# Two-layer hybrid decoder trunk on one core: a later start for the first adding transfers, and two more FFN pairs by seven products

## The chip, the core and the metric

The kernel runs on one core of a Trainium2 chip. The time is device time of one execution in microseconds (us), median of three runs. A core has a matrix engine (TensorE, PE in the profile), a vector engine (VectorE, DVE), a scalar engine (ScalarE, ACT), a general engine (GpSimd, POOL) and a queueing engine (SyncE, SP). Each takes its instructions in its own order and waits on semaphores for the others. Sixteen DMA engines move data; transfers are issued from SP, ACT or POOL, and each of these has a queue of its own on the DMA engines: q1 in the profile is SP's, q10 ACT's, q0 POOL's.

## The reference

x is 512 tokens by 1024 columns, float32. Layer 0 runs latent attention (8 heads) and differential attention (4 heads) in parallel, layer 1 dilated and stick-breaking attention. Each layer ends in a gated convolutional FFN with 2816 hidden columns:

```python
def conv_ffn(h, w_up, conv_w, conv_b, w_down):
    u = causal_dwconv(h @ w_up, conv_w, conv_b)
    gate, up = jnp.split(u, 2, axis=-1)
    return (jax.nn.silu(gate) * up) @ w_down

for i in range(DEPTH):                      # DEPTH = 2
    h = rms_norm(x, pre_g)
    h = even_mixer(h, ...) if i % 2 == 0 else odd_mixer(h, ...)
    x = x + rms_norm(h, post_g)
    h = conv_ffn(rms_norm(x, ffn_pre_g[i]), ...)
    x = x + rms_norm(h, ffn_post_g[i])
```

## The kernel before, in words

**Products.** A float32 operand is split into a high part (a cast to the matrix engine's rounded float32, on ACT) and a low part (the difference, on DVE). A product is three matmuls: high by high, high by low, low by high (`mm3`, lines 315 to 317). For weights these are `wh` and `wl` (lines 81 and 82), made from a raw tile `wraw`. SP loads the raw tiles (lines 57 and 59) in the order of one long list of units, into three buffers; a load waits until the low part of the unit three places earlier is made, for that frees its buffer.

**The stages in order.** `even()`: the combined projections; the latent attention (scores at line 1111, masked by adding `mmask` in the same DVE instruction that finds the maximum, line 895; exponentials on ACT, line 899), with the value products `av` of the differential attention put between its steps; then the differential attention (scores 1227, `alibi` added at 1231, exponentials 1238, combination 1243 to 1245, transposes 906, output 1256, and a normalisation on POOL, 1262 and 1263), with projections for its later heads (`aqk`) as fillers between its steps; then the output projection. `ffn(0)`, `odd()` and `ffn(1)` follow.

**What the differential attention needs first.** When the latent attention's last output is split, ACT issues three loads: `subg` (line 1182), `lamb` (1184) and `alibi` (1188). DVE scales `subg` (1199), forms the lambda sums from `lamb` (1192), then makes the low parts of three weight tiles (82), and then takes the first scores with `alibi` (1231). In ACT's order the first exponentials (1238) stand behind a cast of one more weight tile. The order of these engines in this stage is written out by hand, step by step: score, at most one weight unit, exponentials, fillers, transposes of the step before, output of the step before that.

**The FFN's up product.** The 2816 hidden columns are 22 tiles of gate and up each, worked as 22 pairs. A pair is done directly (two units of weights, 48 matmuls of 512 columns) or, for the pairs in `SEVEN`, by a scheme of seven products of half-size blocks in place of eight (`seven`, 84 matmuls of 256 columns). The scheme needs sums of weight blocks. These sums are not made by the engines but by **adding transfers**: DMAs from DRAM to DRAM, issued by POOL, that copy a block or add it to what is there. A chunk of three pairs takes eight of them, each waiting for those that it builds on:

```python
steps = [(0, 3, ALU.bypass), (2, 2, ALU.bypass), (0, 2, ALU.add), (2, 0, ALU.add), (1, None, ALU.bypass),
         (1, 0, ALU.add), (3, -1, ALU.bypass), (3, 1, ALU.add)]                       # line 161 issues
moves = [lambda c=c, step=step: move(c, *step) for step in steps for c in chunks]
if mark is not None:
    moves.insert(0, lambda: nc.gpsimd.dma_start(tiles[0][chunks[0]][0:1, 0:1], mark)) # line 168
```

A group of moves has no engine that it would naturally wait for. To hold it back until a given moment, `make_sums` puts a **mark** ahead of it: a transfer of one element from a tile that is made at that moment, into the place that the first move overwrites. POOL then waits for the mark's source, and the first move for the mark's landing.

**Where the groups stand.** Chunks 0 to 2 of the first FFN: one group of 24 moves of 768 KB, marked by a normalisation factor of the combined projections (`rk`, line 1074). Chunks 3 and 4: one move after each step of the differential attention. Chunks of the second FFN: one group in `odd()` (line 1494), marked by `lead`. The first FFN has 14 pairs by seven (4 to 17), the second 12 (4 to 15, four chunks). In the stretch by seven the orders of PE, DVE and ACT are written out by hand (line 633 on); a weight unit is made some two to three units ahead of its use.

The tile framework chooses the order of the instructions where no hand-written order is given, from its own estimates, before the kernel runs.

Of the kernel before, what the change touches and what calls it, by code (L numbers as in the profile page):

```python
# [33 lines left out]
PAIRED = [f for k in range(HF) for f in (k, HF + k)]  # L34
TAIL = 4

SEVEN = range(4, 18), range(4, 16)
CHUNK = 3
PAIRS = [len(n) for n in SEVEN]
CHUNKS = [-(-n // CHUNK) for n in PAIRS]  # L40
# [55 lines left out]
def trunk(tc, A, out):  # L96
    nc = tc.nc
    PE, ACT, DVE, POOL = nc.tensor, nc.scalar, nc.vector, nc.gpsimd

    with ExitStack() as top:  # L100
# [28 lines left out]
        lead = cst.tile([P, 80], F32, tag="lead", name="lead")  # L129
# [15 lines left out]
        def sum_steps(layer, chunks, mark=None):  # L145

            wide = "(a q) c -> a (q c)"
            if layer not in sums_of:
                sums_of[layer] = [[dpool.tile([CHUNK * P, S], F32, tag=f"ws{layer}{j}{c}", name="ws")
                                   for c in range(CHUNKS[layer])] for j in range(4)]  # L150
            tiles = sums_of[layer]

            def move(c, j, src, op):
                n = min(CHUNK, PAIRS[layer] - c * CHUNK) * P
                if src is None:
                    src = tiles[0][c][:n]
                elif src < 0:
                    src = tiles[1][c][:n]
                else:
                    src = A[f"ffn_up_q{layer}"][src, c * CHUNK * P:c * CHUNK * P + n]  # L160
                nc.gpsimd.dma_start(tiles[j][c][:n].rearrange(wide, q=4), src.rearrange(wide, q=4), accum_op=op,
                                    max_dma_last_dim=8192)

            steps = [(0, 3, ALU.bypass), (2, 2, ALU.bypass), (0, 2, ALU.add), (2, 0, ALU.add), (1, None, ALU.bypass),
                     (1, 0, ALU.add), (3, -1, ALU.bypass), (3, 1, ALU.add)]
            moves = [lambda c=c, step=step: move(c, *step) for step in steps for c in chunks]
            if mark is not None:
                moves.insert(0, lambda: nc.gpsimd.dma_start(tiles[0][chunks[0]][0:1, 0:1], mark))
            return moves

        def make_sums(layer, chunks, mark):
            with tc.manual_schedule(engines={POOL.engine}):
                for move in sum_steps(layer, chunks, mark):
                    move()
# [13 lines left out]
        def ffn_units(layer):  # L188
            up = []
            for f in range(NF):  # L190
                if f == SEVEN[layer][0]:
                    up += up_blocks(layer)
                elif f not in SEVEN[layer]:
                    up += [(A["ffn_w_up"][layer, f, z], 1024) for z in range(2)]
# [203 lines left out]
        def ffn(layer, xnT, pending, final):  # L398
            with ExitStack() as es:
# [3 lines left out]
                nc.sync.dma_start(cw[:], A["ffn_conv"][layer])  # L403
                pairs = SEVEN[layer]
                minus = cw[:, pairs[0]:pairs[-1] + 1:pairs.step, 1, 0:3]
# [22 lines left out]
                early, hold, homes = [], {}, {}  # L428
# [26 lines left out]
                def x_block(k0, t0):  # L455
                    return [x[:, k0:k0 + 4, t0:t0 + 256] for x in (xh, xl)]
# [91 lines left out]
                def more():  # L548
                    nonlocal ready
                    ready += 1  # L550
                    W.ahead(min(ready, stop))
# [9 lines left out]
                def seven(n, last):  # L561


                    u = begun
                    y = sp.tile([P, 2, S], F32, tag="y", name="y")
                    z1, z2 = u[0][:, :256], u[0][:, 256:]
                    c21, c22 = u[1][:, :256], u[1][:, 256:]
                    p5 = y[:, 1, :256]
                    scale, conv, silu, rest = last
                    heavy = len(rest) > 1  # L570

                    conv(0)
                    more()
                    scale(1)
                    p = bank("t", "p5")[:, :256]
                    product(p, sums[0], True)
                    ACT.copy(p5, p)
                    silu()
                    if heavy:
                        conv(1)  # L580
                    else:
                        more()
                    product(z1, x_block(4, 0), False)
                    product(c21, sums[1], False)
                    DVE.tensor_tensor(z2, c21, p5, ALU.add)
                    if heavy:
                        rest[0]()
                    else:
                        conv(1)
                    more()  # L590
                    if n != pairs[-1]:
                        begin_seven()
                    if heavy:
                        rest[1]()
                    product(c21, sums[2], False)
                    DVE.tensor_tensor(c22, c21, p5, ALU.add)
                    rest[2 if heavy else 0]()
                    product(z2, x_block(4, 256), False)
                    more()
                    product(c21, sums[3], False)  # L600
                    if heavy and n < 2 * (HF - 4) + 2:
                        rest[3]()
                    elif heavy:
                        late.append(rest[3])
                    left = evict(n, y, u)
                    left[0](0)
                    return left
# [14 lines left out]
                for n, f in enumerate(PAIRED):  # L622
                    if n == 2:
                        for i in ORDER:
                            nc.sync.dma_start(spill[i * P:(i + 1) * P, :], X[i][:])
                    if n == (2 if final else 3):
                        for step in x_sums():
                            step()
                    if n == pairs[0]:
                        depth, W.depth = W.depth, 0  # L630
                        ready, stop = W.pos + 3, W.pos + (7 * PAIRS[layer] + 1) // 2 + 2
                        W.ahead(ready)
                        written = tc.manual_schedule(engines={PE.engine, DVE.engine, ACT.engine})
                        written.__enter__()
                        begin_seven()
                    if n in pairs:
                        left = seven(n, left)
                        if n == pairs[-1]:
                            for step in late:
                                step()  # L640
                            finish(left)
                            written.__exit__(None, None, None)
                            W.depth = depth
                        continue
                    u = u4[2 * n:2 * n + 2] if n < 2 else [None] * 2
                    y = sp.tile([P, 2, S], F32, tag="y", name="y")
                    scale, conv, silu, rest = left = evict(n, y, u)
                    for z in range(2):
                        if u[z] is None:
                            u[z] = bank("as"[z], "u")  # L650
                            wh, wl = W.next()
                            for k in range(KD):
                                b = slice(k * P, (k + 1) * P)
                                mm3(u[z], wh[:, b], wl[:, b], xh[:, k], xl[:, k], k == 0, k == KD - 1)
                        if z == 0 or n != pairs[0] - 1:
                            scale(z)
                        if n != pairs[0] - 1:
                            conv(z)
                    if n != pairs[0] - 1:
                        silu()  # L660
                        for step in rest:
                            step()
# [199 lines left out]
        def even():  # L862
            with ExitStack() as es:
# [51 lines left out]
                with ExitStack() as e1:  # L915
# [116 lines left out]
                    with ExitStack() as e2:  # L1032
# [11 lines left out]
                        for i in ORDER:  # L1044
# [9 lines left out]
                            rk = mean_square(a[:, 256:384])  # L1054
# [16 lines left out]
                            split(cT[0][:, :, t], cT[1][:, :, t], tp[:, 0:3])  # L1071
                            ACT.copy(mk[0][64:128, t], tp[64:128, 3])
                            ACT.copy(mk[1][0:64, t], tp[0:64, 3])
                        make_sums(0, range(3), rk[0:1, 0:1])
                        for z in range(2):
                            diff_qk(0, z)
                        ch, cl = cT
# [25 lines left out]
                    sc = e1.enter_context(tc.tile_pool(name="esc", bufs=1, reuse_waits="tile"))  # L1103
                    mmask = sc.tile([P, S], F32, tag="mmask", name="mmask")
                    nc.scalar.dma_start(mmask[:], A["mla_mask"])

                    def score(p2, i, z):
                        def f(_):
# [299 lines left out]
        def odd(xnT, pending, order):  # L1408
            xh, xl = xnT
            with ExitStack() as es:  # L1410
# [80 lines left out]
                DVE.tensor_copy(tri[:], trif[:])  # L1491

                ACT.copy(lead[0:1, 1:2], st[0:1, 0:1])
                make_sums(1, range(CHUNKS[1]), lead[0:1, 1:2])


                for u in range(2):
# [327 lines left out]
def layout(inputs):  # L1825
# [50 lines left out]

    for n, pairs in enumerate(SEVEN):
        q = r["ffn_w_up"][n, pairs[0]:pairs[-1] + 1].reshape(len(pairs), 2, P, 2, S)
# [48 lines left out]
```

## Time and profile before

| | us |
|---|---|
| median of 3 runs | 1135.01 (1134.89 to 1135.72) |
| the profiled execution, its own time | 1134.86 |
| its span, first to last instruction | 1133.1 |
| PE busy | 1115.9 |
| DVE busy | 889.1 |
| ACT busy | 631.5 |
| POOL busy | 108.1 |
| mean granted clock of PE | 0.995 |

In the profile, a row of a timeline reads: start in us from the span's first instruction, duration in us, engine, line, operation, tile written <- tiles read, shapes, count, and in brackets the idle time of the engine before it with what ended it. SPq, ACTq and POOL rows with DMA_DIRECT2D are the issuing of transfers. A row of DMA issues gives the tiles, the queue, the count, the size of one and the median time from issue to landing. A row that begins with a stretch A:B gives its length and the busy time of each engine in it.

### The profile page before, as it was taken

What the parts mean: (1) busy time and instruction counts of PE and PEld (TensorE: products, weight loads), DVE (VectorE), ACT (ScalarE), POOL (GpSimd) and SP (SyncE); (2) the same over time, 40 slices, a digit from 0 to 9 for tenths busy, and PEclk for the clock granted to TensorE, in tenths of its full rate; (3) what the DMA queues carried; (4) which work ended last, traced back from release to release, by engine and by line L of the source; (5) the groups of instructions that cost most, each with busy time, mean ns of one, the idle gap of its engine ahead of it and who ended that gap; (6) DMA issues with size and microseconds to landing.
All of it is one profiled execution on the core that took longest, in us unless ns stands there. A gap on an engine that the chain in (4) does not pass through costs nothing.

```text
span 1133.1 us, 17611 instructions
## 1 busy us (share of the span) xinstructions
PE 1115.9 (98%) x6576; PEld 957.3 (84%) x6576; DVE 889.1 (78%) x1504; ACT 631.5 (56%) x1070; POOL 108.1 (10%) x213
## 2 busy tenths in 40 slices
PE   9979999999999999999999999999999999999997
PEld 8856677789999998888888877888999999888886
DVE  6657566489899999898974476677889999779896
ACT  5445466455566665456653455565466666435662
POOL 2312023320000000000031111102000000000002
PEclk9989999999999999999999999999999999999999
DMA  8799658743355655354637999922236565334461
GB/s 297 268 242 269 183 173 211 176 145 97 118 185 177 195 175 166 98 157 158 227 118 241 313 279 282 281 67 87 98 110 189 184 183 188 113 89 145 147 204 75
DMA packets 66229, 201.48 MB, mean 178 GB/s; under 512 B 9056, under 2 KB 10208, under 8 KB 59360
## 3 DMA queue, kind: packets, MB, share of 16 engines
q1 hardware_dynamic: 56352, 142.09, 38.6%
q0 software_dynamic: 7872, 54.53, 18.7%
q10 hardware_dynamic: 1920, 3.74, 1.1%
q8 instruction: 52, 0.85, 0.3%
q14 instruction: 33, 0.27, 0.1%
HBM read 192.95 MB, written 60.85 MB: 224 GB/s over the span
## 4 chain that ended last, share of the span: by engine, by line
PE 90%; issue 3%; DMA 3%; POOL 1%; DVE 1%; ACT 1%; SPq 0%; POOLq 0%; DVEq 0%; ACTq 0%
PE u L317 12%; PE u L315 12%; PE u L316 12%; PE acc L315 6%; PE acc L317 6%; PE acc L316 6%; PE apt L315 3%; PE apt L316 3%; PE apt L317 2%; PE sps L1111 2%; PE ao L317 1%; PE ao L315 1%; PE ao L316 1%; PE av L317 1%; PE av L316 1%
## 5 line engine op out<-in xcount | busy, mean ns | idle before, releaser
L81 ACT CAST wh<-wraw 128x1024 fp32r<-128x1024 f32 x237 | 245.4, 1048 | 149.0 <-PE u L316 51.3
L82 DVE TENSOR_TENSOR wl<-wraw,wh 128x1024 fp32r<-128x1024 f32 x237 | 287.2, 1219 | 50.7 <-ACT wh L81 50.0
L315 PE MATMUL u<-xh,wh 128*128 128x256 f32 (+1 forms) x664 | 212.0, 319 | 0.0
L316 PE MATMUL u<-xl,wh 128*128 128x256 f32 (+1 forms) x664 | 211.8, 319 | 0.0
L317 PE MATMUL u<-xh,wl 128*128 128x256 f32 (+1 forms) x664 | 211.7, 319 | 0.0
L315 PEld LDWEIGHTS u<-xh,wh 128*128 128x128 f32 x664 | 126.5, 191 | 9.0 <-ACT wh L81 0.3
L317 PEld LDWEIGHTS u<-xh,wl 128*128 128x128 f32 x664 | 126.5, 190 | 8.9 <-DVE wl L82 0.3
L316 PEld LDWEIGHTS u<-xl,wh 128*128 128x128 f32 x664 | 126.5, 190 | 8.7
L317 PE MATMUL acc<-wh,gl 128*128 128x512 f32 (+1 forms) x250 | 96.9, 388 | 0.0
L316 PE MATMUL acc<-wl,gh 128*128 128x512 f32 (+1 forms) x250 | 96.8, 387 | 0.0
L315 PE MATMUL acc<-wh,gh 128*128 128x512 f32 (+1 forms) x250 | 96.8, 388 | 0.0
L317 PE MATMUL u<-gh,wl 128*128 128x256 f32 x312 | 88.3, 283 | 0.0
L315 PE MATMUL u<-gh,wh 128*128 128x256 f32 x312 | 88.3, 283 | 0.0
L316 PE MATMUL u<-gl,wh 128*128 128x256 f32 x312 | 88.3, 283 | 0.0
L230 POOL TENSOR_TENSOR rv<-ms,epst 128x1 f32<-128x1 f32 x39 | 12.1, 309 | 756.0 <-ACT junk L282 369.7
L492 ACT ACTIVATE y<-u,cw 128x512 f32<-128x512 f32 x88 | 67.5, 776 | 14.9 <-PE u L317 14.9
L496 DVE SCALAR_TENSOR_TENSOR y<-u,cw,y 128x511 f32<-128x511 f32 x88 | 65.0, 743 | 5.1 <-ACT y L492 5.1
L498 DVE SCALAR_TENSOR_TENSOR y<-u,cw,y 128x510 f32<-128x510 f32 x88 | 65.5, 746 | 2.3
L315 PEld LDWEIGHTS u<-gh,wh 128*128 128x128 f32 x312 | 59.9, 192 | 0.2
L316 PEld LDWEIGHTS u<-gl,wh 128*128 128x128 f32 x312 | 59.9, 192 | 0.1
L317 PEld LDWEIGHTS u<-gh,wl 128*128 128x128 f32 x312 | 59.9, 192 | 0.0
L315 PEld LDWEIGHTS acc<-wh,gh 128*128 128x128 f32 x250 | 46.9, 188 | 10.1 <-issue 0.5
(363 smaller groups left out, 2437.4 us busy)
## 6 DMA issues: line engine op xcount, KB each, us to landing
ws<-in_ffn_up_q POOLq DMA_DIRECT2D x48, 768.0 KB, 15.3
wraw<-ws SPq DMA_DIRECT2D x104, 256.0 KB, 2.9
wraw<-in_ffn_w_down SPq DMA_DIRECT2D x44, 512.0 KB, 3.5
wraw<-in_ffn_up_q SPq DMA_DIRECT2D x78, 256.0 KB, 2.9
wraw<-in_ffn_w_up SPq DMA_DIRECT2D x36, 512.0 KB, 4.1
ws<-ws POOLq DMA_DIRECT2D x16, 768.0 KB, 16.0
wraw<-in_od_w_dqk SPq DMA_DIRECT2D x12, 512.0 KB, 11.0
wraw<-in_ffn_w_down SPq DMA_DIRECT2D x22, 256.0 KB, 2.9
```

The lines of the kernel that those rows point to most:

```text
L81: self.nc.scalar.copy(h[:, :w], raw[:, :w])
L82: self.nc.vector.tensor_tensor(l[:, :w], raw[:, :w], h[:, :w].bitcast(F32), ALU.subtract)
L230: POOL.tensor_tensor(v[:, :n], ms, epst[:, :n], ALU.add)
L315: PE.matmul(o, lh, rh, start=first, stop=False, skip_group_check=more)
L316: PE.matmul(o, lh, rl, start=False, stop=False, skip_group_check=more)
L317: PE.matmul(o, ll, rh, start=False, stop=last, skip_group_check=more)
L492: ACT.activation(y[:, z], u[z], AF.Identity, bias=c[:, 3:4], scale=c[:, 2:3])
L496: DVE.scalar_tensor_tensor(y[:, z, 1:], u[z][:, :S - 1], c[:, 1:2], y[:, z, 1:], ALU.mult, ALU.add)
L498: DVE.scalar_tensor_tensor(y[:, z, 2:], u[z][:, :S - 2], c[:, 0:1], y[:, z, 2:], ALU.mult, ALU.add)
L1111: PE.matmul(s_ps[:, :w], mq[h][:, i * P:(i + 1) * P], mk[h][:, :w], start=True, stop=True)
```

## The change

Three edits. The first group of adding transfers is marked by the latent mask, when its load has landed, in place of the normalisation factor, and so stands at a later place of the program. The second FFN takes 14 of its pairs by seven products, and so has a fifth chunk (two pairs, moves of 512 KB). The sums of this chunk are made during the first FFN's up product, after its pair 9, marked by an element of a held product that is copied by ACT; the group in `odd()` keeps chunks 0 to 3.

```diff
-SEVEN = range(4, 18), range(4, 16)
+SEVEN = range(4, 18), range(4, 18)
...
                     if n in pairs:
                         left = seven(n, left)
+                        if n == 9 and not final:
+                            ACT.copy(lead[0:1, 2:3], hold[3][0][0:1, 0, 0:1])
+                            make_sums(1, range(4, 5), lead[0:1, 2:3])
                         if n == pairs[-1]:
...
                             ACT.copy(mk[1][0:64, t], tp[0:64, 3])
-                        make_sums(0, range(3), rk[0:1, 0:1])
                         for z in range(2):
                             diff_qk(0, z)
...
                     nc.scalar.dma_start(mmask[:], A["mla_mask"])
+                    make_sums(0, range(3), mmask[0:1, 0:1])
...
                 ACT.copy(lead[0:1, 1:2], st[0:1, 0:1])
-                make_sums(1, range(CHUNKS[1]), lead[0:1, 1:2])
+                make_sums(1, range(4), lead[0:1, 1:2])
```

## The prediction

> **What bounds the kernel now.** I read the page first: TensorE (PE) is busy for 98% of the span and makes up 90% of the chain that ended last.
>
> ```profile
> span 1133.1 us, 17611 instructions
> PE 1115.9 (98%) x6576; PEld 957.3 (84%) x6576; DVE 889.1 (78%) x1504; ACT 631.5 (56%) x1070; POOL 108.1 (10%) x213
> PE 90%; issue 3%; DMA 3%; POOL 1%; DVE 1%; ACT 1%; SPq 0%; POOLq 0%; DVEq 0%; ACTq 0%
> ```
>
> So an edit counts by the PE time that it removes, or by a wait of PE that it ends or makes. Next I read the chain in order of time around the first edit, the timeline of PE there, and a table of stretches (us, PE busy, PEld, DVE, ACT, POOL, granted clock, DMA share, GB/s).
>
> ```profile
> 61.47 11.02 DMA mmask<-in_mla_mask
> ...
> 73.02 2.07 PE L1111 MATMUL sps<-mk,mq 128*128 128x256 f32 x4 [6.83 <-DVE st L895]
> ...
> 66.20:73.00 6.80, 0.00 (x0) 0.00 (x0) 0.34 (x3) 0.00 (x0) 1.33 (x2) 0.87 1.02 261
> 73.00:78.00 5.00, 4.98 (x11) 3.40 (x12) 2.77 (x15) 2.49 (x10) 1.03 (x2) 0.50 1.06 259
> ...
> 75.00:126.00 51.00, 50.91 (x246) 32.45 (x244) 36.51 (x147) 27.61 (x88) 6.51 (x10) 0.97 0.92 237
> 143.00:200.00 57.00, 57.00 (x300) 40.61 (x299) 37.63 (x112) 37.89 (x111) 17.23 (x35) 1.00 0.72 194
> ```
>
> The load of the latent mask takes 11.0 us, PE stands still for 6.8 us behind it, and then works for 5 us at half its clock. The DMA engines are full (1.02) all that time. The rest of the latent attention (75 to 126) and the differential attention (143 to 200) are filled with PE work to the last 0.1 us. The cause is the first group of adding transfers, which POOL issues from 40.05 on:
>
> ```profile
> 36.48 0.75 POOL L168 DMA_DIRECT2D ws<-rr  x1 [0.33 <-POOL rr L233]
> 40.05 3.28 POOL L161 DMA_DIRECT2D ws<-in_ffn_up_q  x6 [2.82 <-DMA ws<-rr]
> 112.61 0.79 POOL L161 DMA_DIRECT2D ws<-in_ffn_up_q  x1 [1.86 <-DMA ws<-ws]
> 149.14 0.19 POOL L1262 TENSOR_TENSOR st<-st,epsp 128x1 f32<-128x1 f32 x1 [35.63 <-ACT jk L1260]
> ```
>
> How the queues share the engines is in the DMA view of short windows (packets, MB, share of the 16 engines' time): first 40 to 125 us (the whole group, on q0), then 65 to 71 (mask on q10, weights on q1), 115.5 to 123 (adds alone), 85.5 to 88 (copies alone).
>
> ```profile
> q0 software_dynamic: 2688, 18.88, 85.3%
> ...
> q0 software_dynamic: 128, 0.89, 71.6%
> q1 hardware_dynamic: 111, 0.45, 20.4%
> q10 hardware_dynamic: 124, 0.25, 10.9%
> ...
> q0 software_dynamic: 205, 1.41, 90.9%
> ...
> q0 software_dynamic: 142, 0.98, 95.8%
> ```
>
> Three things follow. The group needs 0.853 x 85 = 72.5 us of all 16 engines. The three queues got about the same number of packets (128, 111, 124), whatever their size: turn by turn, one packet each. And an adding packet is slow: 7.5 x 16 x 0.909 us over 1.41 MB, that is 172 packets of 8 KB, gives 0.63 us, a copying one 2.5 x 16 x 0.958 over 120 gives 0.32 us. So a small transfer pays one 0.32 to 0.63 us packet of the group for each of its own. The mask (144 packets, 9 on each engine) took nine turns of 0.79 us (0.63 + 0.16), 7.1 us, and 3.9 us of start and landing.
>
> **Edit 1, the group begins at the mask's landing: what it gives.** The same kind of load on the same queue without the group is the smask row; three loads of dqk weights stand beside the mask in either kernel.
>
> ```profile
> smask<-in_sb_mask ACTq DMA_DIRECT2D x1, 256.0 KB, 2.6
> ```
>
> Issued at 61.47, the mask lands at 64.1, or by 65.7 if it takes turns with the weights. PE has value products until 66.2 anyway, so the whole wait of 6.8 us goes, and with it the slow clock: 5.0 us at 0.50 cost at most 2.5, and I take 2.0, since PE had short waits in there. The latent attention then runs **8.8 us earlier**. What is late next in it is PE's own work (the row of 75 to 126).
>
> **What it takes.** POOL's mark now waits for the mask. Behind it in POOL's order stand the 24 moves, a memset and the first normalisation of the differential attention (149.14). By the first two POOL rows, the first move comes 3.6 us after the mark: at 68.0 instead of 40.05. The group then needs its 72.5 us, so it runs until 140.5 at least. In before it was over 1.5 us ahead of the loads of the next stage (last move at 112.61 plus 12.0 to its landing); now these are inside it. This is the transition, first by engine (ACT, DVE, SP, PE), then the landing times of the loads and q10's packets from 126 to 134:
>
> ```profile
> 126.08 0.34 ACTq L1182 DMA_DIRECT2D subg<-in_ev_subln_g  x1
> 136.74 1.05 ACT L81 CAST wh<-wraw 128x1024 fp32r<-128x1024 f32 x1 [2.27 <-DMA wraw<-in_ev_w_dqk]
> 131.60 0.23 DVE L1192 CUSTOM_DVE_ANT_0 lj<-lamb 128x64 f32<-128x64 f32 x1 [2.43 <-DMA lamb<-in_ev_lam]
> 132.02 3.49 DVE L82 TENSOR_TENSOR wl<-wraw,wh 128x1024 fp32r<-128x1024 f32 x3
> 135.50 0.68 DVE L1231 CUSTOM_DVE_ANT_0 s<-sps,alibi 128x512 f32<-128x512 f32 x1
> 139.70 0.75 DVE L1245 SCALAR_TENSOR_TENSOR s<-s,st 128x512 f32<-128x512 f32 x1
> 133.26 0.33 SPq L59 DMA_DIRECT2D wraw<-in_ev_w_dqk  x1
> 140.41 0.92 PE L1227 MATMUL sps<-dqk 64*128 64x384 f32 x4
> 142.75 0.60 PE L906 MATMUL tpp<-ident,s 128*128 128x128 f32 x4
> ...
> alibi<-in_alibi ACTq DMA_DIRECT2D x1, 1024.0 KB, 7.1
> wraw<-in_ev_w_dqk SPq DMA_DIRECT2D x1, 512.0 KB, 3.5
> lamb<-in_ev_lam ACTq DMA_DIRECT2D x1, 128.0 KB, 5.1
> ...
> q10 hardware_dynamic: 432, 1.25, 53.3%
> ```
>
> In before the order is: lamb lands (131.57), DVE goes on to the low parts of the weights (132.02), the first of these frees a raw buffer, SP loads the next weights (133.26 to 136.72), ACT casts them (136.74), and only behind that cast, in ACT's order, come the first exponentials; DVE combines until 140.45, and PE transposes at 142.75, with 2.3 us to spare.
>
> In after the ACT loads are issued at 126.08 - 8.8 = 117.3 and start after about 3.1 us (the mask's 3.9 less its landing), at 120.4. The group has then had 52 us, less some 3 of starts and gaps: 23 us of it are left, which by its order are some ten packets of adds, 18 of copies and 18 of adds on each engine. q10's 432 packets are 27 turns on each engine, with 0.533 x 8 = 4.3 us of its own. lamb is through after 18 turns: 10 x 0.63 + 8 x 0.32 + 1.3 = 10.2 us, with landing at 131; a count with the group 1 us further on gives 129.5. I take 130.5. alibi: nine turns more, 136 to 137. The weights' load is issued 1.7 us after lamb as before, at 132.2, and meets the adds. Loads of that size took 9.8 to 10.9 us beside the group:
>
> ```profile
> wraw<-in_ev_w_dqk SPq DMA_DIRECT2D x1, 512.0 KB, 9.8
> ...
> wraw<-in_ev_w_dqk SPq DMA_DIRECT2D x1, 512.0 KB, 10.9
> ```
>
> With 9.9 it lands at 142.1. Cast to end of combine is 140.45 - 136.74 = 3.7, so PE transposes at 145.8, **3.1 us later** than in before although it came 8.8 earlier. alibi at 136.5 lets DVE's L1231 end at 138, which is ahead of 140.41, so it is not the last gate. PE idles in two pieces, together over 10 us, so the slow clock comes back: +2.0 (0 to 2.5). The row of 143 to 200 has PE full, so nothing is caught up there. Sum of edit 1: **+5.1**, from -8.8 (nothing is held up) to +8 (load 12 us, full dip).
>
> By the Trainium skill ("DMA: Bandwidth & Descriptors", section "Queues, rings and completion order") an engine drains a whole packet of some 9 to 17 descriptors from one ring before it turns to the next. By that rule the small loads would wait for one move's share at a time. The equal counts from 65 to 71 us speak against it; it is the second rival.
>
> **Edit 2, 14 pairs by seven products.** The second FFN's rows (first and last start of the seventh-product matmuls, four to a pair; and of every third matmul of a direct pair):
>
> ```profile
> L315 PE MATMUL p<-gh,wh x48: 283/283/283, 836.0 to 948.0; 128*128 128x256 f32 x48
> L315 PE MATMUL u<-xh,wh x93: 389/389/395, 957.5 to 1020.3; 128*128 128x512 f32 x93
> ```
>
> A pair by seven: (112.0 - 1.1)/11 = 10.08 us. A direct pair is 16 triples of 62.8/92 = 0.683: 10.92. Two pairs: **-1.7 us**. The first FFN does the same 14 pairs now, with PE never idle, so neither weights nor evictions are the limit:
>
> ```profile
> 290.00:433.00 143.00, 143.00 (x1185) 142.41 (x1184) 130.43 (x183) 91.08 (x124) 0.00 (x0) 1.00 0.58 179
> ACT wh L81 <- DMA wraw<-ws: 3.1, 7, 0.7
> ws<-in_ffn_up_q POOLq DMA_DIRECT2D x6, 512.0 KB, 6.8
> ```
>
> **Edit 3, the fifth chunk in the first FFN's up.** One tiny copy on ACT, which is idle for a third of that stretch and whose source was made a pair earlier; one mark and eight moves of 512 KB on POOL, which does nothing there (0.00) until the FFN's tail. At about 6 us each in sequence they run 40 us from about 352. Engine time: four copies of 1.3 and four adds of 2.5. A weight load that meets an add is late by up to 2.5; seven such loads made ACT wait already (at most 0.7) and PE lost nothing. But DVE has only 9% free. I take **+0.5**, from 0 to four adds less DVE's free time, 10 - 3.5, of which I carry +3.
>
> **Sum.** The profiled execution took 1134.86 us, 1.8 more than its span and 0.15 under the median. 1134.9 + 5.1 - 1.7 + 0.5 = **1138.8 us**.
>
> **Rivals.** (a) *Break-even.* The gate at lamb and weights takes up just the 8.8 us: the load lands by 139 (lamb at 129, the load in 8.5 us because the group pauses between its steps), PE transposes at its old time, and only 1.7 less 0.5, plus 0 to 2 of slow clock, remain: 1133.7 to 1135.7. For it: each landing is uncertain by 2 us. Against: the adds fall on the load itself. (b) *Faster.* The loads pass the group: whole moves alternate with whole loads, lamb waits for about 3.8 + 1.9 and the weights for one move; 2 of the 8.8 are lost and no dip comes: 1134.9 - 6.8 - 1.7 + 0.5 = 1127; with nothing held up 1125. It decides if lamb lands before 126. Against: the equal counts and mask's 11.0. (c) *Much slower.* The group stretches so far that POOL's last move, 112.61 + 28 = 140.6, slips past the normalisations (149.14 + 3): every us over 8 is paid by PE; 1143 to 1147. That the mask is still late is unlikely (turns of 0.25 us beside weights alone).
>
> **How the numbers follow.** Forecast 0.50 (own range 1136 to 1142, a fifth of it within 2.3 us of before), (a) 0.22, (b) 0.20, (c) 0.08. A measurement of this kernel can tell about 0.2%, 2.3 us, from no change. Faster: 0.20. Same: (a) and that fifth, 0.32. Slower: 0.48. The range leaves out (c) and most of (b): 1128.0 to 1142.5.
>
> **What would show it.** Edit 1's gain: the mask lands within 4.5 us, PE has no wait of 6.8 us and no half clock near 66. Its price: lamb takes over 10 us from issue, the next weights' load some 10, PE waits for over 8 us before the first transposes of the differential attention, with a half clock behind it. Edit 2: the second FFN's p rows number 56, 10.08 us apart. Edit 3: PE's busy time between 290 and 433 stays whole. The forecast fails if lamb or the weights' load land as fast as alone (5.1 and 3.5), or if DVE takes the weights' low parts ahead of lamb.

## The result

| kernel | time, us (median, range) | ratio to before, 95% interval |
|---|---|---|
| before | 1134.95 (1134.45 to 1135.72, 4 runs) | |
| after | 1143.7 (1142.16 to 1145.82, 4 runs) | 1.0078 [1.0058, 1.0098] |

The change makes the kernel 8.8 us slower. The prediction said slower, 1138.8 us, but its range ended at 1142.5. The profiled execution of after is its fastest run, 1142.16 us, 7.3 more than the profiled one of before. Line numbers of after are up to three higher than those of before.

The page of after, the first two of the three lines that the prediction shows:

```profile
span 1140.3 us, 17809 instructions
PE 1117.0 (98%) x6648; PEld 960.9 (84%) x6648; DVE 893.7 (78%) x1511; ACT 634.8 (56%) x1078; POOL 114.1 (10%) x222
```

PE's busy time is almost the same (1115.9 before), so the 7 us are waits and slower matmuls. The view that names them is the table of waits of PE alone, from 60 to 1100 us (total, times, longest). First before, where the next one is 0.3 us, then after:

```profile
PE sps L1111 <- DVE st L895: 6.8, 1, 6.8
```

```profile
PE sps L1230 <- DVE st L1234: 6.0, 1, 6.0
PE tpp L909 <- DVE s L1248: 4.2, 1, 4.2
PE u L315 <- DVE u L596: 2.2, 1, 2.2
PE u L315 <- DVE u L585: 0.6, 2, 0.4
PE u L315 <- ACT u L559: 0.5, 1, 0.5
```

The wait for the mask is gone. In its place stand two waits at the start of the differential attention (10.2 us together) and four in the first FFN's up (3.3). The first two are edit 1, and this is their timeline in after (POOL, then DVE, SP and ACT, then PE):

```profile
64.79 0.75 POOL L168 DMA_DIRECT2D ws<-mmask  x1 [28.32 <-DMA mmask<-in_mla_mask]
68.38 3.19 POOL L161 DMA_DIRECT2D ws<-in_ffn_up_q  x6 [2.84 <-DMA ws<-mmask]
...
138.84 0.79 POOL L161 DMA_DIRECT2D ws<-in_ffn_up_q  x1 [2.38 <-DMA ws<-ws]
...
130.83 0.23 DVE L1195 CUSTOM_DVE_ANT_0 lj<-lamb 128x64 f32<-128x64 f32 x1 [3.34 <-DMA lamb<-in_ev_lam]
...
131.25 3.49 DVE L82 TENSOR_TENSOR wl<-wraw,wh 128x1024 fp32r<-128x1024 f32 x3
...
132.50 1.47 SPq L59 DMA_DIRECT2D wraw<-in_ev_w_dqk  x2
...
142.83 1.04 ACT L81 CAST wh<-wraw 128x1024 fp32r<-128x1024 f32 x1 [11.26 <-DMA wraw<-in_ev_w_dqk]
...
137.35 2.31 PE L1230 MATMUL sps<-dqk 64*128 64x384 f32 x4 [5.97 <-DVE st L1234]
146.68 1.08 PE L909 MATMUL tpp<-ident,s 128*128 128x128 f32 x4 [4.16 <-DVE s L1248]
```

The chain reads from top to bottom. The mask lands before 64.79, POOL begins the group at 68.38 and issues its last move at 138.84 instead of 112.61. DVE stands for lamb until 130.83, and what it makes next in its order, the low parts of three weight tiles, comes only then (131.25). The first of them frees a raw buffer, so that the next load of weights is issued at 132.50; it lands and is cast at 142.83, and PE transposes at 146.68 instead of 142.75. The stretches of after around this chain (length, PE, PEld, DVE, ACT, POOL, granted clock, DMA share, GB/s) show the clock:

```profile
131.00:137.30 6.30, 0.38 (x2) 0.00 (x0) 4.49 (x12) 0.20 (x1) 1.62 (x2) 0.88 1.02 366
137.30:140.00 2.70, 2.65 (x5) 1.41 (x6) 0.66 (x3) 0.00 (x0) 0.90 (x2) 0.50 1.04 249
...
142.50:146.70 4.20, 0.04 (x2) 0.05 (x1) 2.53 (x5) 2.95 (x6) 0.00 (x0) 0.91 1.01 254
146.70:150.00 3.30, 3.30 (x12) 2.55 (x12) 1.80 (x7) 2.74 (x6) 0.00 (x0) 0.58 1.03 259
```

PE is idle twice, and each time it comes back at about half of its clock, with the DMA engines full (1.01 to 1.04 in these rows) throughout. The loads by their issue rows in after, from 116 to 136 us (count, size, us from issue to landing):

```profile
alibi<-in_alibi ACTq DMA_DIRECT2D x1, 1024.0 KB, 18.4
wraw<-in_ev_w_dqk SPq DMA_DIRECT2D x2, 512.0 KB, 12.8
...
lamb<-in_ev_lam ACTq DMA_DIRECT2D x1, 128.0 KB, 13.5
```

In before these took 7.1, 3.5 and 5.1. (12.8 is the median of two loads; the one of the chain, issued first, was there after 10.3 us.) The third place is the first FFN's up. The same stretch as in the prediction, now in after, and the waits of ACT for weights there (293 to 442 us):

```profile
290.00:433.00 143.00, 139.71 (x1135) 137.94 (x1134) 127.64 (x179) 87.30 (x122) 5.85 (x9) 1.00 0.64 196
```

```profile
ACT wh L81 <- DMA wraw<-ws: 11.7, 6, 4.2
```

PE loses 3.3 us in a stretch that was full, and ACT's longest wait for a weight load has grown from 0.7 to 4.2 us. Edit 2 shows as the prediction had it, 56 rows of seventh products, (132.1 - 1.1)/13 = 10.08 us apart:

```profile
L315 PE MATMUL p<-gh,wh x56: 282/283/284, 845.0 to 977.1; 128*128 128x256 f32 x56
```

By the starts of the first matmuls of each stage, the profiled run of after loses 4.9 us up to the first FFN's up, 4.1 in it, nothing from its down to the second FFN, and wins 1.5 in the second FFN's up.

### The profile page after: what moved, and what is told of

The parts are those of the page before. It is cut to its first block, busy times and chain, and to the rows that moved or that the text cites. A ratio compares the mean times of both kernels' runs of the same rounds, so it can differ in the third digit from the quotient of the medians.

```text
span 1140.3 us, 17809 instructions
## 1 busy us (share of the span) xinstructions
PE 1117.0 (98%) x6648; PEld 960.9 (84%) x6648; DVE 893.7 (78%) x1511; ACT 634.8 (56%) x1078; POOL 114.1 (10%) x222
## 4 chain that ended last, share of the span: by engine, by line
PE 89%; DMA 4%; DVE 3%; issue 1%; ACT 1%; POOL 0%; SPq 0%; POOLq 0%; DVEq 0%; ACTq 0%
PE u L317 11%; PE u L315 11%; PE u L316 11%; PE acc L315 6%; PE acc L316 6%; PE acc L317 6%; PE apt L315 3%; PE apt L316 3%; PE apt L317 2%; PE ao L315 2%; PE ao L317 2%; PE ao L316 2%; PE sps L1114 2%; DMA wraw<-ws 1%; PE aqk L315 1%
## 5 line engine op out<-in xcount | busy, mean ns | idle before, releaser
L315 PE MATMUL u<-xh,wh 128*128 128x256 f32 (+1 forms) x656 | 206.4, 315 | 0.0
L317 PE MATMUL u<-xh,wl 128*128 128x256 f32 (+1 forms) x656 | 206.4, 315 | 0.0
L316 PE MATMUL u<-xl,wh 128*128 128x256 f32 (+1 forms) x656 | 206.3, 314 | 0.0
L315 PE MATMUL u<-gh,wh 128*128 128x256 f32 x336 | 95.6, 284 | 3.3 <-DVE u L596 2.2
L317 PE MATMUL u<-gh,wl 128*128 128x256 f32 x336 | 95.1, 283 | 0.0
L316 PE MATMUL u<-gl,wh 128*128 128x256 f32 x336 | 95.1, 283 | 0.0
L315 PEld LDWEIGHTS u<-gh,wh 128*128 128x128 f32 x336 | 64.4, 192 | 4.2 <-ACT wh L81 2.3
L316 PEld LDWEIGHTS u<-gl,wh 128*128 128x128 f32 x336 | 64.4, 192 | 0.1
L317 PEld LDWEIGHTS u<-gh,wl 128*128 128x128 f32 x336 | 64.4, 192 | 0.0
L161 POOL DMA_DIRECT2D ws<-in_ffn_up_q x60 | 43.1, 721 | 130.2 <-DMA ws<-ws 58.8
```

What stands on the lines that cost most here:

```text
L315: PE.matmul(o, lh, rh, start=first, stop=False, skip_group_check=more)
L316: PE.matmul(o, lh, rl, start=False, stop=False, skip_group_check=more)
L317: PE.matmul(o, ll, rh, start=False, stop=last, skip_group_check=more)
```

## The experiments

My theory after the result: edit 1 costs what the prediction said, edit 2 gives what it said, and the term that was mis-sized is edit 3, because the eight moves delay weight loads in a stretch that has no slack. The rivals: edit 1's late group also spoils the later up; or the moves cost their price in any place; or it is the issuing and the small ACT copy, not the transfers. For all kernels one table, from the starts of the first matmul of each stage in the profiled runs (us): when the first FFN's up begins; how long it takes to the down's first matmul; from there to the second FFN's up; that up to its down.

| kernel | time | up begins | first up | down and odd stage | second up |
|---|---|---|---|---|---|
| before | 1135.0 | 243.5 | 232.2 | 311.8 | 233.5 |
| after | 1143.7 | 248.4 | 236.3 | 311.8 | 232.0 |
| edit 1 alone | 1141.2 | 251.1 | 231.9 | 311.8 | 233.5 |
| edits 2 and 3 alone | 1138.7 | 243.4 | 236.8 | 311.9 | 232.0 |
| fifth chunk in the odd stage | 1144.0 | 243.1 | 232.3 | 322.6 | 232.0 |
| fifth chunk after the seven | 1135.1 | 243.3 | 231.9 | 313.2 | 232.0 |
| fifth chunk in the down | 1139.0 | 244.3 | 231.7 | 318.2 | 232.0 |
| fifth chunk at the start | 1133.4 | 244.3 | 231.9 | 312.1 | 232.1 |
| fifth chunk of copies | 1134.7 | 244.2 | 233.6 | 312.2 | 232.1 |
| lamb early | 1136.7 | 245.1 | 232.4 | 311.7 | 233.6 |
| mask early | 1127.8 | 236.9 | 232.1 | 311.9 | 233.6 |
| mask early, chunk at the start | 1125.7 | 235.8 | 232.3 | 312.4 | 232.0 |

Where nothing ahead of the up was changed, it begins at 243.1 to 244.3; so much a profiled run differs from the next before the places that matter here.

### Edit 1 alone

```diff
-                        make_sums(0, range(3), rk[0:1, 0:1])
...
                     nc.scalar.dma_start(mmask[:], A["mla_mask"])
+                    make_sums(0, range(3), mmask[0:1, 0:1])
```

> Edit 1 alone: the first group of adding moves is marked by the mask's landing; the second FFN keeps 12 pairs by seven and nothing is added in the first FFN's up. Theory: edit 1 and the fifth chunk's sums cost about the same and add up. The first FFN's first direct up matmul comes 4.6 us later than before (273.7 instead of 269.0 in the profiled run), its up takes 206.6 us as before, the second FFN's up 208.2 as before, and the time is 1135.0 + 4.6 = about 1139.6 us. Rival 1, that the first FFN's up is long because of something that edit 1 leaves behind (a later start of the weights, a lower clock): the up takes about 211 us here too, and the time is about 1145. Rival 2, that edit 1 costs nothing by itself: 1135.

Measured: 1141.22 us (1139.70 to 1142.03), ratio 1.0050 [1.0033, 1.0067], that is 3.7 to 7.6 us. The theory's 1139.6 is 1.6 too low. The first FFN's up takes no longer than before, so rival 1 falls; rival 2 falls too. The profiled run has the same chain as after with the lambda load another 2.5 us longer (16.0 us), and its up begins 7.6 us late instead of 4.9. So edit 1 costs 5 to 8 us, and its size differs from run to run with the landing of one small load.

### Edits 2 and 3 alone

```diff
-SEVEN = range(4, 18), range(4, 16)
+SEVEN = range(4, 18), range(4, 18)
...
+                        if n == 9 and not final:
+                            ACT.copy(lead[0:1, 2:3], hold[3][0][0:1, 0, 0:1])
+                            make_sums(1, range(4, 5), lead[0:1, 2:3])
...
-                make_sums(1, range(CHUNKS[1]), lead[0:1, 1:2])
+                make_sums(1, range(4), lead[0:1, 1:2])
```

> Edits 2 and 3 alone: 14 pairs by seven in the second FFN, the fifth chunk's sums inside the first FFN's up, the first group back behind the normalisations where it was before. Theory: the first direct up matmul is at 269 as before, the first FFN's up takes 206.6 + 4.4 = 211 us, the second FFN's up 208.2 - 1.5 = 206.7, and the time is 1135.0 + 4.4 - 1.5 = about 1137.9 us. Rival: the first FFN's up is long because of edit 1; then it takes 206.6 here and the time is about 1133.5.

Measured: 1138.67 us (1137.81 to 1139.98), ratio 1.0034 [1.0021, 1.0047]. The up is 4.6 us longer without edit 1, and the second up 1.5 shorter. The parts add up: 6.1 and 3.6 make 9.7 against 8.8 measured for both, within the intervals.

### Where the eight moves stand: odd stage, end of the seven, down, start

Each of the next four kernels is edits 2 and 3 alone with the fifth chunk's sums at another place. In the odd stage (the group there keeps all five chunks, so the diff is edit 2 only):

```diff
-SEVEN = range(4, 18), range(4, 16)
+SEVEN = range(4, 18), range(4, 18)
```

> Edit 2 alone: 14 pairs by seven in the second FFN, all five chunks of their sums in the odd stage's one group, first group as before. Theory: what edit 3 costs is its place in the first FFN's up. The first FFN's up takes 206.6 us as before, the second FFN's up 206.7, and the time is 1135.0 - 1.5 = about 1133.5 us, if eight more moves in the odd stage's group hold no load up there. Rival: the eight moves cost the same wherever they stand, since they take the queues' time from loads in the odd stage as well: the odd stage becomes 2 to 4 us longer and the time is 1136 to 1138.

Measured: 1144.02 us, ratio 1.0081 [1.0065, 1.0096]. The theory fell here: the moves cost 10.8 us in the odd stage, more than anywhere else. The timeline of PE and SP's rows of that kernel, and SP's rows of before:

```profile
754.89 3.65 PE L1680 MATMUL t<-ident,s 128*128 128x128 f32 x16 [8.21 <-DVE s L1670]
...
733.42 0.33 SPq L1652 DMA_DIRECT2D stat<-st  x1
747.78 0.38 SPq L1653 DMA_DIRECT2D on<-stat  x1
```

```profile
733.79 0.33 SPq L1652 DMA_DIRECT2D stat<-st  x1
738.47 0.38 SPq L1653 DMA_DIRECT2D on<-stat  x1
```

A softmax statistic goes through DRAM there, a store of 16 KB and a load that waits for its landing. In before the group's last move was issued at 718.7, and the store took 4.7 us; in this kernel POOL still issued at 733.8, the store takes 14.3, and PE stands for 8.2 us.

After the last of the fourteen pairs by seven:

```diff
                             finish(left)
+                            if not final:
+                                ACT.copy(lead[0:1, 2:3], hold[3][0][0:1, 0, 0:1])
+                                make_sums(1, range(4, 5), lead[0:1, 2:3])
                             written.__exit__(None, None, None)
```

> As edits 2 and 3 alone, but the fifth chunk's sums are marked after the last of the first FFN's fourteen pairs by seven instead of after the sixth. Theory: the 4.4 us come from weight loads that land late behind the adding moves while the pairs by seven, with eight weight tiles of their own casting per pair, leave little slack; at the end of that stretch the loads have the same need of the queues, so a part of it stays: the first FFN's up takes 207 to 209 us and the time is about 1134 to 1136. Rival 1: the moves cost 4.4 us wherever they stand in the up: 211 us and about 1138. Rival 2: only the sixth pair's place is bad: 206.7 us and 1133.5.

Measured: 1135.14 us, ratio 1.0002 [0.9993, 1.0012]. The first up is not longer at all; a single wait of PE of 1.1 us comes where the down begins, and the stage behind is 1.4 us longer. The time is in the theory's range, but the part that stays stands in the down, not in the up. Rival 1 falls; rival 2 has the up right and the time 1.6 us too low.

In the down, by its third pair of weights:

```diff
+                    if k == 2 and not final:
+                        make_sums(1, range(4, 5), t2[2][0:1, 0:1])
```

> Edit 2 alone, with the fifth chunk's sums marked in the first FFN's down, by the third of its doubled weight sums, where TensorE is fed by loads that hold the queues about half of the time and GpSimd's queue is empty. Theory: the place decides. Eight moves at about 500 to 540 lie beside loads with slack: up 206.6 and down 103.7 us as before, second FFN's up 206.7, and the time is 1135.0 - 1.5 = about 1133.5 us. Rival: the moves cost 1 to 4 us here as well, since each added packet delays a down weight: down 105 to 108 and 1135 to 1138.

Measured: 1138.96 us, ratio 1.0038 [1.0025, 1.0050]: the rival was right in its sign, and its price of 1 to 4 us is exceeded: 6.4 by the starts of the matmuls, all of it in the down, and 5.9 by the times (4.3 slower than before, with edit 2's 1.6 on top). PE's wait of that kernel from 485 to 545 us:

```profile
PE acc L316 <- DVE wl L82: 3.5, 2, 2.3
```

PE waits for low parts of weights, whose loads of 512 KB took 6.3 us instead of 3.9. I had read a queue that is busy half of the time as slack.

At the first FFN's start, beside its direct pairs:

```diff
                 for n, f in enumerate(PAIRED):
+                    if n == 0 and not final:
+                        make_sums(1, range(4, 5), X[ORDER[-1]][0:1, 0:1])
```

> Edit 2 alone, with the fifth chunk's sums marked by the last token block before the first FFN, so that its eight moves lie beside the first FFN's direct pairs (255 to 300 us), where the kernel before moved 0 to 1 MB in 5 us with holes of 5 us, and loads run ahead of their use. Theory: what the moves cost is how little slack the loads beside them have: 4.4 us by the sixth pair by seven, 1.4 us at that stretch's end, 3.8 us in the down, 10.8 us in the odd stage, so here 0 to 1 us: the first FFN's up 206.6 to 207.6 and the time 1135 - 1.6 + 0 to 1 = 1133.4 to 1134.4 us. Rival: eight moves cost 1.4 us or more in every place, and the time is 1135 or above.

Measured: 1133.41 us (1132.58 to 1134.04), ratio 0.9985 [0.9975, 0.9994]. The first up takes 231.9, the second 232.1: here the moves cost nothing that shows, and edit 2's gain is left whole. Its loads beside the moves took 3.7 to 4.0 us instead of 2.9 to 3.0 (medians), and no engine waited for one of them. (The theory names 3.8 us for the down; the table's starts give 6.4.)

The five places in before (start, pair 9, end of the seven, down, odd stage) have DMA shares of 0.30, 0.61, 0.29, 0.43 and 0.98, and the same eight moves cost 0, 4.6, 1.4, 6.4 and 10.8 us there. The two quiet places are the cheap ones, but the order is not that of the shares: the down is dearer than pair 9, although these two windows of before (pair 9, then the down) show its queues less busy:

```profile
352.00:395.00 43.00, 43.00 (x361) 43.00 (x360) 40.34 (x56) 28.92 (x41) 0.00 (x0) 1.00 0.61 188
...
487.00:525.00 38.00, 38.00 (x169) 31.47 (x168) 34.90 (x45) 22.70 (x30) 0.00 (x0) 1.00 0.43 134
```

The order is that of another view, which the prediction read for one place only: the longest wait of ACT or DVE for a weight load, in before, in the same windows. At the start (253 to 290) there is none; then the end of the seven, pair 9, the down and the odd stage (total, times, longest):

```profile
DVE wraw L351 <- DMA wraw<-in_ffn_w_down: 0.3, 1, 0.3
ACT wh L81 <- DMA wraw<-ws: 1.3, 3, 0.7
DVE wraw L351 <- DMA wraw<-in_ffn_w_down: 2.3, 2, 1.5
ACT wh L81 <- DMA wraw<-in_od_w_dqk: 4.5, 1, 4.5
```

None, 0.3, 0.7, 1.5 and 4.5 stand beside costs of 0, 1.4, 4.6, 6.4 and 10.8. Five places in order are a sign and not a proof, and in the odd stage the load that was late was another one, the statistic's.

### The fifth chunk of copies

```diff
+            if plain:
+                steps = [(j, src, ALU.bypass) for j, src, _ in steps]
...
+                            make_sums(1, range(4, 5), lead[0:1, 2:3], True)
```

> Edits 2 and 3 alone, with the four adding moves of the fifth chunk's eight turned into plain copies, which leaves the additions of that chunk out. Same mark, same count of moves and bytes, same places in GpSimd's order; a copied packet of 8 KB took 0.31 us and an added one 0.63 in the runs so far, so the eight moves hold the queues for about two thirds of their time. Theory: what costs 4.4 us is the time that the moves hold the queues while weight loads are due: the first FFN's up falls from 211.0 to about 208 to 209 us and the time from 1138.7 to about 1136. Rival: the ScalarE copy, the issuing on GpSimd or the eight transfers' mere number cost it: 211 us and 1138.7 as with additions.

Measured: 1134.65 us, ratio 0.9999 [0.9989, 1.0008]. This kernel leaves out the additions, so only its time is read. The same mark, as many moves and the same bytes at the same place cost 1.4 us instead of 4.6. So it is the time that the moves hold the DMA engines, and the rival falls. How that becomes PE time is one event in each kernel. In edits 2 and 3 alone the third and fourth move of the chunk, which both add, are in flight together (POOL). A load of weights is issued just before them, at 362.81; ACT waits for it and casts it, DVE makes its low part, and only behind that, in DVE's order, comes the addition that PE waits for (ACT, DVE, PE):

```profile
363.48 0.82 POOL L161 DMA_DIRECT2D ws<-in_ffn_up_q  x1 [6.31 <-DMA ws<-in_ffn_up_q]
364.61 0.78 POOL L161 DMA_DIRECT2D ws<-in_ffn_up_q  x1 [0.31 <-DMA ws<-in_ffn_up_q]
...
371.59 1.04 ACT L81 CAST wh<-wraw 128x1024 fp32r<-128x1024 f32 x1 [4.66 <-DMA wraw<-ws]
...
372.67 1.23 DVE L82 TENSOR_TENSOR wl<-wraw,wh 128x1024 fp32r<-128x1024 f32 x1 [2.70 <-ACT wh L81]
373.81 0.43 DVE L596 TENSOR_TENSOR u<-u,y 128x256 f32<-128x256 f32 x1
...
374.38 0.36 PE L315 MATMUL u<-gh,wh 128*128 128x256 f32 x1 [2.59 <-DVE u L596]
```

The rows of this load's issue in before, in edits 2 and 3 alone, in after and in the kernel of copies, and then PE's wait in the kernel of copies:

```profile
wraw<-ws SPq DMA_DIRECT2D x1, 256.0 KB, 2.9
...
wraw<-ws SPq DMA_DIRECT2D x1, 256.0 KB, 8.7
...
wraw<-ws SPq DMA_DIRECT2D x1, 256.0 KB, 8.3
...
wraw<-ws SPq DMA_DIRECT2D x1, 256.0 KB, 7.2
...
PE u L317 <- DVE u L598: 1.1, 1, 1.1
```

The load is 5.8, 5.4 and 4.3 us late, and PE waits 2.6, 2.2 and 1.1: each time 3.2 less. That is the slack of this load; ACT, upstream of PE, waits for 4.7, 4.2 and 3.1.

### Lamb early

Edit 1 alone, with the lambda vector loaded ahead of the group:

```diff
                     nc.scalar.dma_start(mmask[:], A["mla_mask"])
+                    lamb = dqk[3][:, 0, 0:256].rearrange("p (a b) -> p a b", a=4)
+                    nc.scalar.dma_start(lamb, A["ev_lam"].partition_broadcast(P))
+                    make_sums(0, range(3), mmask[0:1, 0:1])
...
-                lamb = sc.tile([P, 4, 64], F32, tag="lamb", name="lamb")
-                nc.scalar.dma_start(lamb[:], A["ev_lam"].partition_broadcast(P))
```

> Edit 1 alone, with the lambda vector loaded right behind the mask, ahead of the group, into a slice of the fourth head's query and key tile that is free until then. Theory: under the group the lambda load takes 13 to 16 us and ScalarE, which waits for the exponential of its sums, casts no weights and so releases no next weight load until about 131; the weight load then lands at 143 and TensorE waits 4 us for it. With the lambda there early the next weight load is issued at about 120 instead of 132.5, that second wait of TensorE (4.0 us in edit 1 alone) goes with half of its clock dip, and the wait for alibi, 6 to 8 us, stays: the time falls from 1141.2 by 4 to 6, to about 1135 to 1137 us. Rival: alibi decides alone and takes longer still because the weight load now lies beside it: 1140 to 1142.

Measured: 1136.69 us (1135.31 to 1138.33), ratio 1.0018 [1.0008, 1.0027], 4.5 us less than edit 1 alone (4.1 when each is taken against the runs of before beside it). Its timeline (DVE and ACT, then PE):

```profile
128.84 0.23 DVE L1199 TENSOR_SCALAR subg<-subg 128x128 f32<-128x128 f32 x1 [7.53 <-DMA subg<-in_ev_subln_g]
...
138.11 1.05 ACT L81 CAST wh<-wraw 128x1024 fp32r<-128x1024 f32 x1 [11.47 <-DMA wraw<-in_ev_w_dqk]
...
135.45 1.58 PE L1227 MATMUL sps<-dqk 64*128 64x384 f32 x4 [2.69 <-DVE st L1231]
141.97 1.09 PE L906 MATMUL tpp<-ident,s 128*128 128x128 f32 x4 [2.68 <-DVE s L1245]
```

The time came as expected, the way only in part: the weight load was issued at 130.2, not at 120, and both waits of PE became shorter (4.0 to 2.7 and 7.8 to 2.7) instead of one of them going. The expectation had the wrong engine for the gate. ACT has cast its three tiles by 125.8 here and by 124.4 in edit 1 alone, long before; it is DVE that stands, in edit 1 alone for lamb (until 133.4) and here for the next small load, subg (64 KB, 10.5 us, until 128.84), and with it the low parts that free the buffer. So the lambda load is a gate of edit 1's price, worth 4 to 4.5 us; behind it stands subg, and the group on the queues keeps a part of the rest through alibi and the weights.

### Mask early

The kernel before with one change: the mask is loaded on SP behind the rope table, into a part of a tile that is free until the differential attention. The group keeps its place.

```diff
+                        mmask = dqk[3][:, 0]
+                        nc.sync.dma_start(mmask, A["mla_mask"])
...
-                    mmask = sc.tile([P, S], F32, tag="mmask", name="mmask")
-                    nc.scalar.dma_start(mmask[:], A["mla_mask"])
```

> The kernel before with one thing changed: the latent mask is loaded on SyncE behind the rope table, into a part of the fourth head's tile that is free until the differential stage, so that it lands before the group; the group keeps its mark and place, the second FFN its 12 pairs. Theory: the wait of 6.8 us at 66 to 73 and the half clock behind it, 2.0 us, go, and nothing takes their place since the group still ends before the differential loads: first direct up matmul at about 260 instead of 269, 1135.0 - 8.8 = about 1126 us. Rival: about 9 us earlier the differential loads fall into the end of the group, whose last moves were issued at 112.6, as in edit 1: lambda and alibi take 8 to 12 us and half of the gain is lost, 1129 to 1132.

Measured: 1127.84 us (1127.30 to 1128.72), ratio 0.9939 [0.9924, 0.9954], 6.8 us faster than before. Its stretch from 62 to 74 us, where before had the wait, is full at full clock, although three weight loads issued there took 10 to 20 us beside the group: no one was due for them. At the next stage one wait is left:

```profile
136.44 0.63 PE L906 MATMUL tpp<-ident,s 128*128 128x128 f32 x4 [1.33 <-DVE s L1245]
```

The theory's 8.8 less this 1.3 is 7.5, of which the times show 6.8; the other 0.7 was not located. The loads do meet the group's tail, as the rival had it (lamb took 9.4 us, alibi 11.4), but less than a quarter of the gain is lost.

### The best of both

The early mask, 14 pairs, and the fifth chunk at the first FFN's start (the diffs of these two kernels together).

> The early mask with the group at its old place, together with 14 pairs in the second FFN and the fifth chunk's sums at the first FFN's start: the parts of the change that the runs have shown to gain, without the places that cost. Theory: the two gains add up, 1135 - 6.9 - 1.6 + 0 to 1 = 1126.5 to 1127.5 us. Rival: with the first FFN some 7 us earlier the eight moves meet the tail of the first FFN's sums and its first weight loads, and the time is that of the early mask alone, 1127.8, or above.

Measured: 1125.68 us (1124.15 to 1126.23), ratio 0.9914 [0.9900, 0.9928], a little below the theory's 1126.5. The gains add up, and this version beats both kernels: 9.3 us faster than before, 18.0 faster than after.

## Why the prediction was wrong, point by point

- **Edit 1, what it gives: right.** The mask landed 2.7 us after its issue, the wait of 6.8 us and the half clock near 66 are gone. ACT issues the loads of the next stage from 116.98 on instead of 126.08, that is 9.1 us earlier where 8.8 was predicted. The early mask, which takes only this part, is 6.8 us faster; the row of 1.33 accounts for most of the difference from 8.8.
- **Edit 1, what it takes: right in mechanism and nearly in size.** First move 68.0 predicted and 68.38 measured; lamb at 130.5 and 130.8 (117.35 + 13.46 by the table of issues); next weights issued at 132.2 and 132.50, cast at 142.1 and 142.83; transposes at 145.8 and 146.68. The price was +5.1 in the sum; the profiled runs show 4.9 and 7.6, the timed ones 6.1. That alibi is no gate was right for the transposes and wrong for PE's first wait: DVE's L1234 with alibi holds the scores for 6.0 us. By the chain above this wait lay ahead of the transposes, so it changed the clock and not the sum; no run tests it. The landing of lamb was counted turn by turn, one packet of each queue. It came within 0.3 us of the count in after, but 2.9 later than the count in edit 1 alone (133.4), so the closeness is partly luck. The turns themselves are in the trace: cut into half microseconds, which is less than one adding packet of 0.63, q0 and q10 pass nearly the same number of packets each time (in after from 121.5 on: 25 and 25, 7 and 9, 15 and 13). That speaks against a queue that drains many descriptors at a time, the rule of the Trainium skill's "DMA: Bandwidth & Descriptors" ("Queues, rings and completion order") that the prediction weighed.
- **Edit 2: right.** -1.7 predicted, -1.5 in the stage.
- **Edit 3: wrong, and this is the step that failed.** The term was +0.5, "from 0 to four adds less DVE's free time, 10 - 3.5, of which I carry +3". Measured: 4.1 to 4.6 us, inside the 0 to 6.5 that the step itself had as bounds, but the value was taken at the wrong end and the range was cut at 3. Two things in it were wrong. First, "a weight load that meets an add is late by up to 2.5" counts one add; the chunk's third and fourth moves both add and run together, and the load that met them was 5.4 to 5.8 us late. Second, that ACT already waited up to 0.7 us for loads while PE lost nothing was read as a sign that lateness costs nothing. It was a sign that the slack was partly used: 3.2 us were left, and whatever went beyond them PE waited for. The way to PE led through DVE's order, where the next addition stands behind the late tile's low part; the prediction named what is queued behind a wait for edit 1 and not here. Also a clock dip was not counted, which edits 2 and 3 alone show behind their wait: 2.6 us of wait and about 1.7 of slow clock make up 4.3 of their 4.6.
- **The sum.** With the sizes from the experiments: 1135.0 + 6.1 - 1.6 + 4.1 to 4.6 = 1143.6 to 1144.1, against 1143.7 measured. Of the 4.9 us by which the forecast was too low, edit 3 makes 3.6 to 4.1 and edit 1 about 1.
- **The rivals.** Break-even and faster did not come: the loads did not pass the group. The much slower case did not come in its mechanism: POOL's last move was issued at 138.84, and the first normalisation ran 15 us later. The time of 1143 to 1147 that it gave was reached by another way.

What stays open: the longest waits for loads put the five places in order, but no run shows how to get the price of a place from them, and the slack was measured at pair 9 alone. Of the 4.1 us that after loses in the up, 3.3 are idle time of PE. An estimate for most of the other 0.8: the matmuls there start 0.12 us apart and last 0.28, so a wait costs 0.16 more than the idle time that the view counts, and four waits 0.6.

## What to carry to other kernels

A background transfer costs what the transfers beside it lack in slack, and a full engine without waits does not show that slack: look at the waits for loads one step upstream, on the engines that convert the weights (here 0.7 us of ACT), compare places by them, and take any that are there as a sign that slack is being used up. When a small load is late behind a long group of transfers, move the small load ahead of the group, not the group behind the load; the group meets the next small load otherwise, and when one small load is out of its way, look for the next one in the same engine's order (here subg behind lamb). Where a term has wide bounds and nothing in the trace fixes it, carry both bounds into the range.

## What the runs showed of the hardware

PE's clock fell after a shorter pause than I had expected. The stretches behind the wait of edits 2 and 3 alone (PE idle for 2.6 us until 374.4), behind a wait of 2.3 us in the kernel with the fifth chunk in the down, and behind the first wait of 2.7 us in lamb early:

```profile
374.40:377.00 2.60, 2.60 (x13) 2.60 (x14) 1.50 (x2) 1.72 (x2) 0.00 (x0) 0.55 0.85 310
377.00:380.00 3.00, 3.00 (x23) 3.00 (x22) 2.96 (x5) 2.63 (x5) 0.77 (x1) 0.82 0.89 254
```

```profile
517.30:520.00 2.70, 2.70 (x12) 2.24 (x13) 1.27 (x2) 1.34 (x2) 0.77 (x1) 1.00 0.57 130
```

```profile
135.40:138.00 2.60, 2.55 (x8) 1.45 (x9) 0.67 (x3) 0.00 (x0) 1.01 (x2) 0.94 0.97 402
138.00:139.30 1.30, 1.29 (x4) 0.47 (x2) 0.11 (x1) 1.19 (x2) 0.30 (x1) 0.50 1.18 441
```

A wait of 2.6 us was followed by 0.55 and 0.82 of the clock, about 1.7 us lost; waits of 2.3 (the second fence) and 2.2 (after, in the up) by none. In lamb early the clock fell to 0.50 only 2.6 us after the wait had ended. So the length of a pause alone does not say when the clock falls, and these runs fix no limit. The Trainium skill ("TensorE: Matmul & The Clock Gate", Part 1) puts the return to half clock after at least one idle window of about 3.4 us, with windows that run free of the kernel. Here 2.6 us were enough, and the measurement decides.

The other point is the price of adding: beside the weight loads of pair 9, eight moves of 512 KB cost 4.6 us of PE time when four of them add, and 1.4 when all of them copy.
